# A state-space scan in pairs of chunks, with the matmuls of the scan in written order and its part-array products gathered

## The chip, the cores and the metric

The kernel runs on one core of a Trainium2 chip. The metric is device time in microseconds for one launch. The core's engines are TensorE (PE in the profile: matmuls, with PEld for the loading of weights), VectorE (DVE), ScalarE (ACT), GpSimd (POOL) and SyncE (SP, which issues most DMAs). Each engine works its own instructions off in the order in which they were issued, and waits on semaphores where it needs the result of another.

## The reference

One step of a small hybrid decoder: one Mamba-2 (SSD) layer, then one layer of causal pooling, then an RMSNorm. There are 1024 prompt tokens and 8 sampled sequences of 8 tokens, d_model is 1024, all in float32. The part that matters here is the SSD layer, cut:

```python
def ssd_scan(x, dt, A, B, C, h0):          # T = 128 tokens a chunk, 8 groups of 4 heads, D_STATE 128
    acum = jnp.cumsum(dt * A.reshape(G, R), axis=2)
    decay = jnp.where(mask, jnp.exp(acum[t] - acum[s]), 0.0)
    CB = einsum(C, B); xdt = x * dt
    y_intra = einsum(CB * decay, xdt)                       # inside a chunk
    chunk_states = einsum(B, exp(acum[-1] - acum), xdt)     # S: what a chunk adds to the state
    h = exp(acum[-1]) * h + chunk_states                    # from chunk to chunk
    y_inter = einsum(C, exp(acum), h_prev)                  # from the state before
    return y_intra + y_inter, h_final

def ssd_branch(h, ...):
    z, xbc, dt_raw = split(h @ w_in)
    xs, Bm, Cm = split(silu(conv_b + sum(xp[:, k:k + L] * conv_w[k] for k in range(4))))
    y, new_ssm = ssd_scan(xs, softplus(dt_raw + dt_bias), -exp(a_log), Bm, Cm, ssm_prev)
    gated = (y + d_skip * xs) * silu(z)
    gated = gated * rsqrt(mean(gated * gated over the 256 channels of a group) + EPS) * norm_g
    return gated @ w_out, ...
```

The pooling layer has another silu(z) gate. Both layers take their shift, scale and gate from `silu(c) @ ada_w` (adaLN).

## The kernel before

Activations lie transposed, 128 channels on the partitions and the 1088 tokens (1024 prompt, 64 sample) along the free axis. A float32 product is made as three products of the form float32r: weights and activations are split into a high part (a copy on ScalarE) and a low part (a subtraction on VectorE). Small products in the scan are plain float32, which the hardware does in two passes, so each stands twice in the profile.

**Stages.** `front` norms the input, makes some z, B, C and x projections, and the dt terms (`dt_phase`). `ssd_layer` then runs the scan of the 8 groups g, one after the other, and between their steps the projections of the next group: 4 tiles (B, C, and two of x) of 3 token ranges each, 12 units of 24 matmuls (`proj_group`, `mm1`, L174 to L176). After each tile follow the conv of 4 taps and the silu (`conv_tile`, L340 to L348), written as x/2 * (1 + tanh(x/2)). `ssd_out` and `pool_layer` follow; their large products are made in the seven products of Strassen's scheme.

**The scan of a group** (`scan_group`). For each of 8 chunks, `front(c)` transposes x and B (L534), makes C·B (L530), the decay matrix M (ScalarE Relu L541 and Exp L542, VectorE L545), xd (x times dt, and times the decay to the chunk's end, L547) and C times exp(acum) (ea, L560). `back(c)` makes y (L575 and, from the state before, L579), and the state: S (L582) goes to PSUM, GpSimd multiplies the state before by the decay (hd, L588), and VectorE adds S (L589; for the first chunk a copy, L585). The row of cumulated decays, spread over the partitions, comes by DMA (acb, two buffers). After the chunks come the sample tokens: Z (L603) with the cached states, y (L616, L619), and the new states (`state_sample`: L640, L641 into the PSUM tile S or y, L643 adds on VectorE). Then the gate: y * silu(z) (L671), squares on ScalarE (L672), their sum (L673), the norm's mean by products with ones (L681), Ln and Exp, a trip through DRAM to spread it over the partitions, and the scaling (L693).

**Part of the array.** y, Z, the mean, the sample's transposes (`dup`, L422) and the adaLN products (L245) use 64 or 32 columns of the array with a tile position; two or four of them run side by side. Transposes, C·B, S, the sample's new states and the projections use all of it.

**PSUM.** There are eight banks: mm three, tr two, y two, S one.

```python
S = pp.tile([P, 512], F32, tag="S", bufs=1, name=self.name("S"))                                   # back(c)
S = pp.tile([P, 512], F32, tag=("S", "y")[b2 % 2], bufs=1 + b2 % 2, name=self.name("S"))           # state_sample
```

**Order.** The code is traced once; a planner then orders each engine's instructions by when their inputs are ready in its own plan and, among ready ones, by the order of tracing. It may put a matmul that is traced later ahead of one that waits. In `ssd_layer` a loop gives the tracing order: one step of the scan, one unit of projection.

```python
for g in range(7):
    G = self.proj_open(g + 1)
    sc, pr = self.scan_group(g, T), self.late(self.proj_group(G), sc)
    T = G["out"]
    if g < 6:
        self.weave(itertools.islice(sc, 11), pr, (1, 1, 1, 1, 1, 1, 1, 1, 1, 1, 2))
```

With the last group the units are those of the output product (`out_units`, L1139 to L1141, 24 matmuls of 272 columns a unit).

ScalarE's functions need a table; Exp and Ln share one, tanh is loaded again in turn (L299, L345).

## Time and profile before

| | |
|---|---|
| median of 3 timed runs | 1656.93 us (1655.12 to 1659.39) |
| span of the profiled execution | 1652.6 us |
| TensorE busy | 1606.9 us, 97% |
| VectorE, ScalarE, GpSimd busy | 1348.5, 852.7, 482.3 us |
| DMA | 272.35 MB, mean 165 GB/s |
| mean granted TensorE clock | 0.993 |

The profile gives the profiled execution no time of its own beside its span; the timed runs lie 2.5 to 6.8 us above that span. Rows of a group read: line, engine, operation, output <- inputs, shapes, count | busy us, mean ns of one | idle of the engine before them, and what ended it. A row of the windows: window, its length, then for each engine busy us (and instructions), granted clock, DMA share, GB/s. A row in order of time: start, length, engine, line, operation; in brackets idle time before it and what ended it. A TensorE instruction's length includes its way through the array, so the cost of one in a stream is the distance of the starts. A line number is that of the kernel before.

### The profile page before, as it was taken

The numbers are of one execution on the slowest core, as the hardware profiler recorded it, in microseconds if no ns is written. First come the engines' busy times: TensorE is split into PE (matmuls) and PEld (weight loads), VectorE is DVE, ScalarE is ACT, GpSimd is POOL, SyncE is SP. The second block draws the span as 40 slices with busy tenths as digits, with TensorE's granted clock in tenths as the row PEclk, the third lists the DMA queues.
The fourth block names the chain that finished last, engine by engine and source line by source line (L and its number), as shares of the span: only waits on it lengthen the run. The fifth ranks groups of instructions, "written<-read, shape, count | busy, mean of one in ns | idle before, by whom it ended". The sixth has DMA issues, their size and how long they took to land. (4 is left out here: it accounts for less than half of the span.)

```text
span 1652.6 us, 31547 instructions
## 1 busy us (share of the span) xinstructions
PE 1606.9 (97%) x12255; PEld 1516.0 (92%) x12255; DVE 1348.5 (82%) x2303; ACT 852.7 (52%) x1651; POOL 482.3 (29%) x517
## 2 busy tenths in 40 slices
PE   8999999999999999999888999999999999999997
PEld 6899999888888989888777999999999999999997
DVE  5897587788888787878888988979999878577876
ACT  6544335767676666767665356633332334233364
POOL 0124441213121313223221122256667640000241
PEclk8999999999999999999999999999999999999999
DMA  8423226445555454538897983133323369556773
GB/s 341 161 75 114 85 76 218 135 145 173 161 168 175 148 162 133 173 119 243 260 284 233 240 201 124 56 111 113 112 93 103 126 203 379 168 152 181 163 166 121
DMA packets 120837, 272.35 MB, mean 165 GB/s; under 512 B 18256, under 2 KB 58608, under 8 KB 120688
## 3 DMA queue, kind: packets, MB, share of 16 engines
q1 hardware_dynamic: 112624, 244.91, 44.2%
q0 software_dynamic: 8064, 25.43, 8.5%
q8 instruction: 96, 1.57, 0.4%
q14 instruction: 53, 0.43, 0.1%
HBM read 208.99 MB, written 56.86 MB: 161 GB/s over the span
## 5 line engine op out<-in xcount | busy, mean ns | idle before, releaser
L1139 PE MATMUL op<-b,w 128*128 128x272 f32 x896 | 259.5, 291 | 6.6 <-ACT w L1099 4.3
L1141 PE MATMUL op<-b,w 128*128 128x272 f32 x896 | 259.5, 291 | 3.2 <-DVE w L1100 3.0
L1140 PE MATMUL op<-b,w 128*128 128x272 f32 x896 | 259.2, 290 | 3.4 <-DVE b L1040 3.4
L174 PE MATMUL mm<-hh,wh 128*128 128x364 f32 x720 | 248.8, 346 | 0.0
L175 PE MATMUL mm<-hl,wh 128*128 128x364 f32 x720 | 238.6, 331 | 0.0
L176 PE MATMUL mm<-hh,wl 128*128 128x364 f32 x720 | 237.5, 330 | 0.0
L888 PE MATMUL st<-hh,w 128*128 128x272 f32 x704 | 203.5, 289 | 0.5 <-DVE w L168 0.5
L887 PE MATMUL st<-hl,w 128*128 128x272 f32 x704 | 203.3, 289 | 0.0
L886 PE MATMUL st<-hh,w 128*128 128x272 f32 x704 | 203.1, 288 | 0.0
L1139 PEld LDWEIGHTS op<-b,w 128*128 128x128 f32 x896 | 169.4, 190 | 8.6 <-ACT w L1099 5.0
L1140 PEld LDWEIGHTS op<-b,w 128*128 128x128 f32 x896 | 169.4, 189 | 6.0 <-DVE b L1040 4.1
L1141 PEld LDWEIGHTS op<-b,w 128*128 128x128 f32 x896 | 169.3, 189 | 4.9 <-DVE w L1100 4.2
L888 PE MATMUL st<-t,w 128*128 128x272 f32 x528 | 152.3, 288 | 2.8 <-POOL w L168 2.0
L887 PE MATMUL st<-t,w 128*128 128x272 f32 x528 | 152.2, 288 | 0.7 <-DVE t L1331 0.7
L588 POOL TENSOR_TENSOR hd<-h,cd 128x256 f32<-128x256 f32 x56 | 76.5, 1367 | 261.2 <-DVE h L589 147.3
L886 PE MATMUL st<-t,w 128*128 128x272 f32 x528 | 151.9, 288 | 0.0
L174 PEld LDWEIGHTS mm<-hh,wh 128*128 128x128 f32 x720 | 135.4, 188 | 6.0 <-ACT raw L404 2.5
L175 PEld LDWEIGHTS mm<-hl,wh 128*128 128x128 f32 x720 | 135.5, 188 | 4.2 <-issue 2.7
L342 DVE SCALAR_TENSOR_TENSOR raw<-raw,cwh,raw 128x1112 f32<-128x1112 f32 x96 | 133.0, 1385 | 6.9 <-ACT raw L340 6.4
L176 PEld LDWEIGHTS mm<-hh,wl 128*128 128x128 f32 x720 | 135.3, 188 | 3.0 <-issue 2.9
L886 PEld LDWEIGHTS st<-hh,w 128*128 128x128 f32 x704 | 132.9, 189 | 0.3 <-issue 0.3
L888 PEld LDWEIGHTS st<-hh,w 128*128 128x128 f32 x704 | 132.5, 188 | 0.7 <-DVE w L168 0.7
(289 smaller groups left out, 4208.4 us busy)
## 6 DMA issues: line engine op xcount, KB each, us to landing
wr<-win SPq DMA_DIRECT2D x48, 512.0 KB, 3.7
acb<-acd SPq DMA_DIRECT2D x64, 256.0 KB, 4.3
wr<-pin SPq DMA_DIRECT2D x32, 512.0 KB, 3.9
wr<-wout SPq DMA_DIRECT2D x28, 512.0 KB, 7.8
wr<-pout SPq DMA_DIRECT2D x28, 512.0 KB, 4.2
row<-gyd SPq DMA_DIRECT2D x22, 544.0 KB, 7.9
wr<-wout POOLq DMA_DIRECT2D x20, 512.0 KB, 8.4
wr<-pout POOLq DMA_DIRECT2D x20, 512.0 KB, 5.5
```

The lines of the kernel that those rows point to most:

```text
L174: nc.tensor.matmul(ps[:, :n], hi[:, k, :], ah[:, a:a + n], start=first, stop=False)
L175: nc.tensor.matmul(ps[:, :n], hi[:, k, :], al[:, a:a + n], start=False, stop=False)
L176: nc.tensor.matmul(ps[:, :n], lo[:, k, :], ah[:, a:a + n], start=False, stop=last)
L342: nc.vector.scalar_tensor_tensor(out=acc[:, :n], in0=raw[:, k:k + n], scalar=w[k], in1=acc[:, :n], op0=ALU.mult, op1=ALU.add)
L588: nc.gpsimd.tensor_tensor(out=hd, in0=h, in1=cd.unsqueeze(2).to_broadcast([P, 4, 64]), op=ALU.mult)
L886: nc.tensor.matmul(ps[c][:, :QUART], hi[:, k], xh[:, t], start=(k == 0), stop=False)
L887: nc.tensor.matmul(ps[c][:, :QUART], hi[:, k], xl[:, t], start=False, stop=False)
L888: nc.tensor.matmul(ps[c][:, :QUART], lo[:, k], xh[:, t], start=False, stop=(k == 3))
L1139: nc.tensor.matmul(ps[:, :QUART], hi[:, k], xh, start=k == 0, stop=False)
L1140: nc.tensor.matmul(ps[:, :QUART], hi[:, k], xl, start=False, stop=False)
L1141: mm = nc.tensor.matmul(ps[:, :QUART], lo[:, k], xh, start=False, stop=k == 7)
```

## The change

The scan works on pairs of chunks: 4 steps p of 256 tokens instead of 8 of 128. Its transposes, M, ea, xd, S and y are made for both chunks at once (M and ea 128 x 1024, one tile px for x, one pb for B and C·B); acb is one buffer of twice the size. `scan_front(p + 1)` is issued before the step p.

Every matmul traced in `ssd_layer` is pinned behind the one traced before it on TensorE, so the planner can't reorder them. Each step issues whole-array products first and then all that use a part of the array: y, then the sample's products or the mean, then an adaLN block. The projections of the next group run 3 units ahead (`LEAD`), and `PACE` says how many units stand at three places of each step.

The conv's last tap writes the result directly, and a silu on ScalarE is applied in place, in a burst for all four tiles of a group at the end of a scan; the gates' tanh and multiplication become one silu. The sum of the squares is taken by the products with ones (two sets of them) instead of VectorE. The scale 0.5 and its helper tiles go. The x tiles of the first output product are loaded one by one.

```diff
+LEAD = 3
+PACE = (((1, 1, 1), (0, 1, 2), (0, 1, 2), (0, 1, 2)),) * 6 + (((1, 1, 1), (0, 1, 2), (0, 2, 2), (0, 2, 4)), ((1, 1, 1), (0, 1, 1), (0, 1, 1), (0, 1, 1)))
...
+    def pin(self, ins):
+        return self.build.tc.keep_in_program_order(ins) if self.build.pinned else ins
...
-        for k in range(1, 4):
+        for k in range(1, 3):
             nc.vector.scalar_tensor_tensor(out=acc[:, :n], in0=raw[:, k:k + n], scalar=w[k], in1=acc[:, :n], op0=ALU.mult, op1=ALU.add)
+        nc.vector.scalar_tensor_tensor(out=dst[:, :NP], in0=raw[:, 3:3 + NP], scalar=w[3], in1=acc[:, :NP], op0=ALU.mult, op1=ALU.add)
...
-        nc.scalar.activation(raw[:, :n], acc[:, :n], AF.Tanh)
-        nc.vector.scalar_tensor_tensor(out=dst[:, :NP], in0=raw[:, :NP], scalar=1.0, in1=acc[:, :NP], op0=ALU.add, op1=ALU.mult)
...
+    def silu_burst(self, ts):
+        for t in ts:
+            self.tab(self.nc.scalar.activation(t, t, AF.Silu))
+        self.tab(self.nc.scalar.preload_act_table_set("natural_log_exp_and_others"))
...
+    def scan_state(self, s, p):
+        S = self.pp.tile([P, 512], F32, tag="S", bufs=1, name=self.name("S"))
+        for cc in range(2):
+            self.te.matmul(S[:, 256 * cc:256 * cc + 256], Bt[:, cc], xd[:, cc, 1].rearrange("p r q -> p (r q)"), start=True, stop=True)
+        for cc in range(2):
+            h, Sv = s.h[-1], S[:, 256 * cc:256 * cc + 256].rearrange("p (r q) -> p r q", r=4)
+            if h is None:
+                nc.vector.tensor_copy(hn, Sv)
             else:
+                nc.gpsimd.tensor_tensor(out=hd, in0=h, in1=cd[:, :, cc].unsqueeze(2).to_broadcast([P, 4, 64]), op=ALU.mult)
+                nc.vector.tensor_tensor(out=hn, in0=hd, in1=Sv, op=ALU.add)
...
+    def sample_state(self, s, half):
+        for i in range(2):
+            S = self.pp.tile([P, 512], F32, tag=("S", "y")[i], bufs=1 + i, name=self.name("S"))
+            self.te.matmul(S, Bt[:, 0], xm, start=True, stop=False)
+            self.te.matmul(S, Bt[:, 1], xm, start=False, stop=True)
+            self.nc.vector.tensor_tensor(out=d, in0=d, in1=S, op=ALU.add)
...
+    def gate_norm(self, s):
+        for q in range(2):
+            for j in range(4):
+                self.te.matmul(ps[32 * j:32 * j + 32, :272], self.ones[:, :32], sq[q][:, 272 * j:272 * j + 272], start=(q == 0), stop=(q == 1), tile_position=(0, 32 * j))
...
-        t = self.mt.tile([P, 416], F32, tag="mt", bufs=2, name=self.name("zt"))
-        nc.scalar.activation(t[:, :n], src, AF.Tanh, scale=0.5)
-        return nc.vector.scalar_tensor_tensor(out=dst[:, a:a + n], in0=t[:, :n], scalar=1.0, in1=src, op0=ALU.add, op1=ALU.mult)
+        return self.nc.scalar.activation(dst[:, a:a + n], src, AF.Silu)
...
+    def scan(self, s, fill):
+        for p in range(4):
+            a, b, c = PACE[g][p]
+            if p == 0 and g == 7:
+                self.sample_state(last, 0)
+            self.units(fill, a)
+            if p < 3:
+                self.scan_front(s, p + 1)
...
+            self.scan_state(s, p)
+            if last and p == 0 and g < 7:
+                self.sample_state(last, 0)
+            self.units(fill, b)
+            self.scan_y(s, p)
+            if p == 3:
+                self.sample_y(s)
+            if p == 2:
+                self.sample_front(s)
+                self.sample_inter(s)
+            if last and p == 1:
+                self.gate_norm(last)
+            ada = self.ada(g, p)
+            next(ada, None)
+            if last and p == 0:
+                self.sample_state(last, 1)
...
+            elif p == 3:
+                if g < 6:
+                    self.silu_burst(after.T)
+                self.sample_prep(s)
...
+            self.units(fill, min(c, 1))
...
+            self.units(fill, c - min(c, 1))
+            if p == 3 and after:
...
+                self.scan_front(after, 0)
+                self.scan_ac(after, 1)
+                self.gate_rows(s)
```

## The prediction

> **What bounds the kernel now.** I read the page first, then the sums by window, then the order of TensorE's instructions in the scan, and last the rows of the operations that the change moves.

> ```profile
> span 1652.6 us, 31547 instructions
> PE 1606.9 (97%) x12255; PEld 1516.0 (92%) x12255; DVE 1348.5 (82%) x2303; ACT 852.7 (52%) x1651; POOL 482.3 (29%) x517
> 300.00:750.00 450.00, 450.00 (x3413) 397.77 (x3412) 359.46 (x599) 304.14 (x680) 108.94 (x161) 1.00 0.50 156
> 750.00:900.00 150.00, 133.71 (x1049) 118.68 (x1047) 130.62 (x227) 94.61 (x196) 38.03 (x38) 0.98 0.83 255
> ```

> TensorE (PE) is the bound. In the stage that the change rewrites, 300 to 750 us, it is busy for 450.00 of 450 us; VectorE (359.46) and ScalarE (304.14) have room. So two things can move the time: how long TensorE's own stream takes, and new waits inside it. Only the tail of the scan, 750 to 900 us, has idle time now, 16.3 us. The sum below is made against this execution, span 1652.6 us; the three timed runs have a median of 1656.93, 4.3 us more, which I add at the end.

> A busy PE hides what its instructions cost, so I look at their starts.

> ```profile
> 281.17 0.66 PE L575 MATMUL y<-M,xd 128*64 128x128 f32 x8
> 281.76 0.43 PE L175 MATMUL mm<-hl,wh 128*128 128x360 f32 x1
> ...
> 539.38 0.44 PE L575 MATMUL y<-M,xd 128*64 128x128 f32 x4
> ...
> 540.09 0.39 PE L579 MATMUL y<-ea,h 128*64 128x128 f32 x4
> 540.40 0.70 PE L582 MATMUL S<-xd,Bt 128*128 128x256 f32 x2
> ...
> 546.60 0.70 PE L582 MATMUL S<-xd,Bt 128*128 128x256 f32 x2
> 546.94 0.52 PE L174 MATMUL mm<-hh,wh 128*128 128x364 f32 x1
> 547.30 0.33 PE L175 MATMUL mm<-hl,wh 128*128 128x364 f32 x1
> ...
> 550.94 0.33 PE L176 MATMUL mm<-hh,wl 128*128 128x364 f32 x1
> 551.20 0.27 PE L530 MATMUL tr<-xbc,xbc 128*64 128x64 f32 x1
> ...
> 884.52 0.67 PE L681 MATMUL ms<-z,ones 128*32 128x272 f32 x8
> 885.12 0.39 PE L1140 MATMUL op<-b,w 128*128 128x272 f32 x1
> ```

> The form 128*64 or 128*32 marks a product on part of the array, 128*128 one on all of it. A part stretch of 8 products lasts from 281.17 to 281.76, 0.59 us; one of 16 (four groups of 4, the first and the last shown) from 539.38 to 540.40, 1.02 us. So a product costs 0.054 us, and each stretch 0.16 us that does not depend on its length. The whole-array stretch from 546.60 to 551.20 lasts 4.60 us. It holds 24 projection products at 0.165 us ((550.94 - 547.30) / 22), 3.97 us, and two 256-column passes at 0.215 us (four times 0.054), 0.43 us: 0.20 us are left over. A change of array form and back thus costs about **0.35 us** of TensorE in which nothing is computed, though the engine counts as busy. Between 281.17 and the last such stretch at 884.52 I count 117 part stretches, 14 to 16 for each of the 8 scans.

> **The change part by part.**

> *Four stretches a scan.* In each step of two chunks the change puts y, and whatever of the sample's products, the norm and the adaLN block is due, behind one another. That makes 32 stretches and one for the last norm, 33: 84 fewer, times 0.35 = **-29.4 us**. A quarter of a scan more or less is 2 stretches; bounds -26 and -33. Changes between 64 and 32 columns inside a stretch stay about as many as now (some 3 a scan); I take 0, bounds -2 and +3.

> *Norm.* The squares' sum moves from VectorE to TensorE: 8 more L681 products a scan. The stretch at 884.52 has 8 in 0.60 us, 0.45 without its change of form; 8 x 0.45 = **+3.6 us**, bounds 3 and 5.

> *Other products* (transposes, C·B, S, the sample's, the 84 projection units) stay in number and size: 0.

> *VectorE and ScalarE.*

> ```profile
> L342 DVE SCALAR_TENSOR_TENSOR raw<-raw,cwh,raw 128x1112 f32<-128x1112 f32 x96 | 133.0, 1385 | 6.9 <-ACT raw L340 6.4
> L346 DVE SCALAR_TENSOR_TENSOR xbc<-raw,raw 128x1024 f32<-128x1024 f32 x32 | 40.8, 1274 | 10.2 <-ACT raw L345 10.0
> L348 DVE SCALAR_TENSOR_TENSOR xbc<-raw,raw 128x64 f32<-128x64 f32 x32 | 6.9, 217 | 0.0
> L340 ACT ACTIVATE raw<-raw,cwh 128x1112 f32<-128x1112 f32 x32 | 42.1, 1315 | 1.8 <-DVE xbc L348 1.3
> L404 ACT ACTIVATE raw<-mm 128x364 f32<-128x364 f32 (+1 forms) x84 | 37.6, 449 | 53.7 <-PE mm L176 52.9
> L345 ACT ACTIVATE raw<-raw 128x1112 f32<-128x1112 f32 x32 | 36.2, 1131 | 23.4 <-DVE raw L342 23.3
> L299 ACT ACT_TABLE_LOAD x12 | 15.4, 1283 | 11.5 <-PE ms L681 11.4
> L673 DVE TENSOR_TENSOR z<-z,z 128x1088 f32<-128x1088 f32 x8 | 10.2, 1279 | 0.0
> L754 DVE SCALAR_TENSOR_TENSOR z<-zt,z 128x272 f32<-128x272 f32 x48 | 27.2, 572 | 9.6 <-ACT zt L753 9.5
> L754 DVE SCALAR_TENSOR_TENSOR pz<-zt,pz 128x272 f32<-128x272 f32 x56 | 24.5, 439 | 13.7 <-ACT zt L753 13.7
> ```

> The third full tap goes (32 x 1.385), L673 goes (10.2) and most of L754 goes (51.7 in these two groups): VectorE loses about 106 us. It hides behind TensorE, so the gain is 0, bounds -4 (short waits in the front and pool stages) and 0. ScalarE swaps a tanh for a silu at the same length and keeps about two table loads a scan: 0.

> *Burst against the next scan.* Scan g+1's first transposes need all four silus. From the end of a group's last projection unit to these transposes stand, by the prices above, S (1.1), a unit (4.0), y (1.9), the sample's y (0.9) and two units (8.0), 16 us. The chain is two evictions L404 0.9, L340 1.3, taps 2 x 1.385 + 1.274 + 0.217 = 4.3, table load 1.3, silu 1.1 = 8.9 us: hidden by 7 us; if VectorE is late it comes out into the open. Bounds 0 and +3 at each of 7 borders. The last border has two output units (6 us) instead: about 3 to 6 us, in place of waits that stand there now.

> *One buffer for S, and a fixed order.* Here I expect the loss. In the first step of scans 1 to 6 the code issues `scan_state(s, 0)` and right behind it `sample_state(last, 0)`. Both write the PSUM tile S, which has one buffer, and the matmuls can no longer pass each other. The second must wait until VectorE has copied the first state, GpSimd has decayed it, and VectorE has added the second one. Everything on TensorE is queued behind it. Now only the copy has to be awaited, and the order fills the time:

> ```profile
> 510.40 0.68 PE L582 MATMUL S<-xd,Bt 128*128 128x256 f32 x2
> 512.57 0.41 DVE L585 COPY h<-S 128x256 f32<-128x256 f32 x1
> 512.91 0.40 PE L640 MATMUL S<-xs,Bt 128*128 128x512 f32 x1
> 513.16 0.61 POOL L588 TENSOR_TENSOR hd<-h,cd 128x256 f32<-128x256 f32 x1 [11.56 <-DVE h L585]
> ...
> 587.75 0.42 DVE L585 COPY h<-S 128x256 f32<-128x256 f32 x1
> L585 DVE COPY h<-S x8: 410/417/425, 275.0 to 824.9; 128x256 f32<-128x256 f32 x8
> L588 POOL TENSOR_TENSOR hd<-h,cd x56: 612/932/2817, 281.7 to 865.7; 128x256 f32<-128x256 f32 x56
> L588 POOL TENSOR_TENSOR hd<-h,cd 128x256 f32<-128x256 f32 x56 | 76.5, 1367 | 261.2 <-DVE h L589 147.3 <-DVE h L585 76.8 <-ACT cd L559 23.6
> L589 DVE TENSOR_TENSOR h<-hd,S x56: 404/411/422, 287.8 to 870.1; 128x256 f32<-128x256 f32 x56
> ```

> S ends at 511.08 and the copy starts at 512.57, 1.5 us behind other VectorE work. Then 0.4 (copy), 0.2, 1.4 (mean of L588), 0.3 (half a mean VectorE operation, 1348.5 us / 2303), 0.4 (add), 0.1: 4.3 us, six times that is **+26 us**. Lower bound, with no queue and L588 at its shortest: 0.1 + 0.4 + 0.1 + 0.6 + 0.1 + 0.4 + 0.1 = 1.8, +11 us. Upper bound: L588 at 2.8 and the queue of 1.5 before both VectorE steps, 6.9, +41. I take the middle since at that moment VectorE holds a conv tile (4.3 us), M, ea, and the xd of two steps. `sample_state(last, 1)` then waits in the same step for the two y evictions (its other buffer holds the adaLN block): about 0.7 us, **+4**, bounds 0 and +16 (2.7 each).

> *The clock.* An idle of that length can cost more than itself:

> ```profile
> 824.19 0.58 PE L530 MATMUL tr<-xbc,xbc 128*128 128x128 f32 x1 [3.60 <-ACT Bt L551]
> 826.00:828.00 2.00, 2.00 (x17) 1.64 (x14) 2.00 (x5) 1.27 (x4) 0.88 (x1) 0.50 0.27 62
> 900.03 0.39 PE L1140 MATMUL op<-b,w 128*128 128x272 f32 x1 [3.07 <-DVE b L1040]
> 900.00:904.00 4.00, 3.97 (x30) 3.84 (x31) 4.00 (x7) 1.96 (x3) 1.66 (x2) 1.00 0.93 284
> ```

> After a wait of 3.60 us the granted clock is 0.50 in 826 to 828; after one of 3.07 us it stays 1.00. At half clock for some 4 us or more, 2 us or more are lost. My 4.3 us is a mean; I let half of the six stalls pay 2 us: **+6**, bounds 0 and +20. [...]

> *Tail.* Scan 7 now overlaps its step's front with the step before, so the waits of L530 on Bt (3.60 above) should go; but its acb is one buffer of 512 KB for two of 256 KB, reloaded only after ScalarE has read it:

> ```profile
> acb<-acd SPq DMA_DIRECT2D x64, 256.0 KB, 4.3
> ```

> If a load of twice the size lands in twice the time, 8.6 us, and that only after the reading, it fills the 10 us or so of a step with two output units, and the DMA share there is 0.83 already. I take 0, bounds -10 and +10.

> **Sum.** 1652.6 - 29.4 + 3.6 + 26 + 4 + 6 = 1662.8 of span; with 4.3, **1667 us**, 0.6% slower. Own range 1660 to 1676.

> **The rivals.**

> *Faster: the S chain is short.* VectorE is 106 us lighter and TensorE's halt lets it drain. At the lower bound, without y waits and clock: 1652.6 - 29.4 + 3.6 + 11 = 1637.8, **1642 us**. It decides from the point where a first step loses less than 25.8 / 6 = 4.3 us in all. For it: L588's shortest 0.61 us, and it was 0.61 in the row above. Against it: the copy's 1.5 us of queue.

> *No change.* First steps lose about 4.3 us, all in: **1657 us**, within 5 us of the time before. 0.3% is about what a measurement of this kernel tells from no change.

> *Much slower: every stall halves the clock.* Six times 3.4 us instead of +6, so +20: 1652.6 - 29.4 + 3.6 + 26 + 4 + 20 = 1677, **1681 us**; a burst that is late at the scan borders would give a like time. For it: 4.3 is above the 3.60 that fell. Against: 3.07 did not fall.

> *The change doesn't do what it says*: if a change of form cost nothing, the 25.8 us would be missing and the time be 1693. The rows of 8 and 16 products speak against it; I give it a part of the third rival.

> **How the numbers follow.** Forecast 0.37, faster 0.36, no change 0.12, much slower 0.15. The forecast is ahead by a hair, because the order is written down and the chain has three steps, while its length is an estimate. So faster by over 0.3% is 0.36, within 0.3% 0.13 (a little of the forecast's lower end), slower 0.51. The range runs from 1638 to 1687: below it lies about a third of the faster case, above it half of the much slower one.

> **What will show it.** Right: PE waits on "h" before the sample's S product in scans 1 to 6, 4 to 5 us each, some with a PEclk of 0.5 behind them; about 33 part stretches; VectorE near 1240 us busy. Wrong: no such wait, or below 3 us, and scans that follow each other faster than the 75.2 us of now (587.75 - 512.57) by nearly 4 us; or waits of transposes on silu, which would move the loss to the scan borders. If the tail from 750 us on loses much less than 16 us, my 0 for it was the error.

## The result, and the profile after

The changed kernel takes **1724.49 us** in the median of four runs (1723.92 to 1729.07), beside 1657.7 us for the kernel before: 1.0409 times as long, interval 1.0393 to 1.0425. The forecast was 1667 us with a range up to 1687, so the direction was right and the size far off. The profiled execution has a span of 1722.3 us, 69.7 more than before.

The page of the changed kernel:

```profile
span 1722.3 us, 30963 instructions
PE 1602.7 (93%) x12335; PEld 1536.5 (89%) x12335; DVE 1240.8 (72%) x1984; ACT 831.5 (48%) x1485; POOL 450.5 (26%) x516
```

Its waits of TensorE (what waited, its releaser, microseconds in all, how often, the longest):

```profile
PE S L98 <- DVE h L576: 45.4, 6, 7.9
PE y L98 <- DVE h L576: 29.3, 16, 3.9
PE tr L101 <- ACT xbc L394: 5.9, 1, 5.9
PE S L98 <- DVE h L699: 4.8, 1, 4.8
```

VectorE is 107.7 us lighter (106 were worked out), and TensorE busy 93% instead of 97%. (All of TensorE's products now stand in one line, L98; the sample's S product is "S<-xm", scan_state's "S<-xd".) The first two waits, which are new, make 74.7 us.

I sum TensorE's time over the whole execution from the trace and its clock records: idle time; time lost at half clock, an estimate: half of the time for which TensorE was busy at 0.50 (in the trace after, projection products start 0.305 us apart there and 0.166 us at full clock, output products 0.227 and 0.125, in the median, so the true loss is somewhat below half); and the rest, taken as what its instruction stream needs at full clock. The 4 us of the prediction for y's evictions stand under "all else", since they are another wait than y's on h.

| | before | after | difference | predicted |
|---|---|---|---|---|
| stream | 1597.5 | 1569.5 | -28.0 | -25.8 |
| idle: S on h | 0 | 45.4 | +45.4 | +26 |
| idle: y on h L576 | 0 | 29.3 | +29.3 | 0 |
| idle: all else | 45.7 | 44.9 | -0.8 | +4 |
| half clock | 9.4 | 33.2 | +23.8 | +6 |
| span | 1652.6 | 1722.3 | +69.7 | +10.2 |

One scan shows it in one row each. The windows run from a halt of S to the next in the kernel after, and from a copy to the next in the kernel before; the columns are start and end, length, busy time of PE, PEld, DVE, ACT and POOL with their instructions, granted clock, DMA share, GB/s. After:

```profile
456.92:542.57 85.65, 74.31 (x577) 69.05 (x577) 54.54 (x76) 48.89 (x100) 12.57 (x28) 0.96 0.42 136
```

Before:

```profile
512.57:587.75 75.18, 75.18 (x568) 66.72 (x567) 61.13 (x101) 51.42 (x116) 20.26 (x27) 1.00 0.49 155
```

A scan was 75.18 us, all of it busy at full clock. It is now 85.65, of which 11.3 us are idle and 2.3 are lost to the clock (74.31 busy; the sum of lost time gives a stream of 72.0).

**Where the halt comes from.** The timeline of the changed kernel around the first halt, first TensorE (start, length, engine, line, operation; in brackets the idle time before and its releaser):

```profile
361.27 1.03 PE L98 MATMUL S<-xd,Bt 128*128 128x256 f32 x4
369.95 2.04 PE L98 MATMUL S<-xm,Bs 128*128 128x512 f32 x4 [7.65 <-DVE h L576]
```

GpSimd:

```profile
368.73 0.61 POOL L575 TENSOR_TENSOR hd<-h,cd 128x256 f32<-128x256 f32 x1 [10.77 <-DVE h L572]
```

VectorE:

```profile
361.69 1.37 DVE L358 SCALAR_TENSOR_TENSOR raw<-raw,vec,raw 128x1112 f32<-128x1112 f32 x1
362.98 0.68 DVE L541 TENSOR_TENSOR xd<-tr,tkx 128x512 f32<-128x512 f32 x1
363.58 1.27 DVE L359 SCALAR_TENSOR_TENSOR xbc<-raw,vec,raw 128x1024 f32<-128x1024 f32 x1
364.77 0.28 DVE L361 SCALAR_TENSOR_TENSOR xbc<-raw,vec,raw 128x64 f32<-128x64 f32 x1
364.97 0.68 DVE L541 TENSOR_TENSOR xd<-tr,tkx 128x512 f32<-128x512 f32 x1
365.57 0.41 DVE L544 TENSOR_TENSOR cb<-tr,kc 128x256 f32<-128x256 f32 x1
365.90 1.22 DVE L558 TENSOR_TENSOR ea<-xbc,ea 128x1024 f32<-128x1024 f32 x1
367.03 1.22 DVE L557 TENSOR_TENSOR M<-M,cb 128x1024 f32<-128x1024 f32 x1
368.17 0.42 DVE L572 COPY h<-S 128x256 f32<-128x256 f32 x1
369.38 0.42 DVE L576 TENSOR_TENSOR h<-hd,S 128x256 f32<-128x256 f32 x1 [0.79 <-POOL hd L575]
```

S is done at 362.3. The copy that frees the bank starts at 368.17, **5.9 us** later, behind a convolution tile's taps, two xd, cb, ea and M. After that the chain is short: copy, 0.61 us of decay, add, 1.8 us in all until the next S product at 369.95. TensorE has nothing else to do in this time, because everything is queued behind S<-xm.

The wait of y has the same cause, one step on. TensorE:

```profile
393.07 0.44 PE L98 MATMUL y<-ea,h 128*64 128x128 f32 x4 [1.51 <-DVE h L576]
```

VectorE:

```profile
390.07 1.22 DVE L557 TENSOR_TENSOR M<-M,cb 128x1024 f32<-128x1024 f32 x1
391.21 1.28 DVE L359 SCALAR_TENSOR_TENSOR xbc<-raw,vec,raw 128x1024 f32<-128x1024 f32 x1
392.40 0.28 DVE L361 SCALAR_TENSOR_TENSOR xbc<-raw,vec,raw 128x64 f32<-128x64 f32 x1
392.60 0.41 DVE L576 TENSOR_TENSOR h<-hd,S 128x256 f32<-128x256 f32 x1
```

y needs the state that the step's first chunk adds, one projection unit (4.0 us) stands between S and y, and the add is queued behind M and the taps. Steps 1 and 2 of each scan lose some 1.5 us so, and the last steps up to 3.9.

### The profile page after: what moved, and what is told of

Read it like the earlier page. It is cut to its first block, busy times and chain, and to the rows that moved or that the text cites. A ratio compares the mean times of both kernels' runs of the same rounds, so it can differ in the third digit from the quotient of the medians.

```text
span 1722.3 us, 30963 instructions
## 1 busy us (share of the span) xinstructions
PE 1602.7 (93%) x12335; PEld 1536.5 (89%) x12335; DVE 1240.8 (72%) x1984; ACT 831.5 (48%) x1485; POOL 450.5 (26%) x516
## 4 chain that ended last, share of the span: by engine, by line
PE 68%; DVE 13%; ACT 7%; issue 6%; DMA 5%; POOL 2%; SPq 0%; DVEq 0%; POOLq 0%; ACTq 0%
PE st L98 27%; PE mm L98 18%; PE op L98 13%; DVE raw L358 3%; PE pl L98 3%; DVE xbc L359 2%; PE y L98 2%; PE am L98 2%; PE S L98 1%; ACT M L553 1%; DVE M L557 1%; DVE xd L541 1%; PE ms L98 1%; DMA row<-gyd 1%; DVE wl L153 1%
## 5 line engine op out<-in xcount | busy, mean ns | idle before, releaser
L98 PE MATMUL op<-b,w 128*128 128x272 f32 x2688 | 353.8, 293 | 11.9 <-ACT w L1136 5.9
L98 PEld LDWEIGHTS op<-b,w 128*128 128x128 f32 x2688 | 347.1, 192 | 18.7 <-ACT w L1136 6.6
L98 PE MATMUL st<-hh,w 128*128 128x272 f32 x1408 | 273.8, 289 | 0.0
L98 PE MATMUL mm<-hh,wh 128*128 128x364 f32 x720 | 247.1, 343 | 0.1
L98 PE MATMUL mm<-hl,wh 128*128 128x364 f32 x720 | 239.2, 332 | 0.0
L98 PE MATMUL mm<-hh,wl 128*128 128x364 f32 x720 | 238.6, 331 | 0.0
L98 PEld LDWEIGHTS st<-hh,w 128*128 128x128 f32 x1408 | 224.6, 188 | 0.3 <-issue 0.3
L98 PE MATMUL st<-t,w 128*128 128x272 f32 x1584 | 205.3, 287 | 0.0
L98 PE MATMUL st<-hl,w 128*128 128x272 f32 x704 | 203.4, 289 | 0.0
L98 PEld LDWEIGHTS st<-t,w 128*128 128x128 f32 x1584 | 201.0, 188 | 0.0
L98 PEld LDWEIGHTS mm<-hh,wh 128*128 128x128 f32 x720 | 138.1, 192 | 9.2 <-issue 6.7
L98 PEld LDWEIGHTS mm<-hl,wh 128*128 128x128 f32 x720 | 137.8, 191 | 1.4
L98 PEld LDWEIGHTS mm<-hh,wl 128*128 128x128 f32 x720 | 137.6, 191 | 0.0
L98 PEld LDWEIGHTS st<-hl,w 128*128 128x128 f32 x704 | 132.6, 188 | 0.0
L553 ACT ACTIVATE M<-acb,tka 128x128 f32<-128x128 f32 x256 | 83.0, 390 | 37.6 <-PE y L98 34.8
L1156 DVE SCALAR_TENSOR_TENSOR x<-op,gat,x 128x272 f32<-128x272 f32 (+1 forms) x160 | 72.7, 477 | 37.7 <-PE op L98 31.6
L1136 ACT ACTIVATE w<-wr 128x1024 fp32r<-128x1024 f32 x56 | 59.1, 1055 | 80.7 <-PE op L98 57.6
L358 DVE SCALAR_TENSOR_TENSOR raw<-raw,vec,raw 128x1112 f32<-128x1112 f32 x64 | 87.7, 1371 | 7.7 <-ACT raw L356 7.2
L575 POOL TENSOR_TENSOR hd<-h,cd 128x256 f32<-128x256 f32 x56 | 41.1, 734 | 197.9 <-DVE h L576 111.5
```

What stands on the lines that cost most here:

```text
L98: return self.pin(self.build.nc.tensor.matmul(*a, **k))
L358: nc.vector.scalar_tensor_tensor(out=acc[:, :n], in0=raw[:, k:k + n], scalar=w[k], in1=acc[:, :n], op0=ALU.mult, op1=ALU.add)
L553: nc.scalar.activation(M[:, r, t], acb[:, r, t], AF.Relu, bias=self.tka[cc][:, col + r:col + r + 1], scale=-1.0)
L575: nc.gpsimd.tensor_tensor(out=hd, in0=h, in1=cd[:, :, cc].unsqueeze(2).to_broadcast([P, 4, 64]), op=ALU.mult)
L1136: self.nc.scalar.activation(hi, r, AF.Copy)
L1156: ins = nc.vector.scalar_tensor_tensor(out=x[e][:, a:a + pn], in0=ps[:, :pn], scalar=g, in1=x[e][:, a:a + pn], op0=ALU.mult, op1=ALU.add)
```

## The experiments

The theory after the traces: TensorE's products can no longer pass each other, so each step of VectorE on which a product depends must be on time; the two places where it is not are the shared bank S and the single unit ahead of y. The rivals: VectorE's backlog itself is the loss, wherever the waits stand; or gathering the part-array products brought nothing, and the stream changed for another reason. The kernel before took 1657.45 us beside the first four kernels, 1658.1 beside the others.

### 1. The sample's product first

```diff
-            if p == 0 and g == 7:
+            if last and p == 0:
                 self.sample_state(last, 0)
...
-            if last and p == 0 and g < 7:
-                self.sample_state(last, 0)
```

> The changed kernel, with one line moved: in step 0 of scans 1 to 6 the sample's first new state is issued before the projection unit and scan_state, as it is in scan 7. Nothing is left out. Theory A (one S buffer in a fixed order): the six waits of 7.6 us on VectorE's second state go, 45 us, and the half clock behind them, about 1.8 us each, 11 us. But the chain copy, decay, add starts 5 us late behind VectorE's other work, so y of step 0, one unit (4 us) behind, should now wait 2 to 4 us: 6 x 3 = 18 us come back. 1724 - 45 - 11 + 18 = 1686 us. Theory B (the state chain itself is too late, whoever reads it): the wait moves to y whole, but for the unit between, so 7.6 - 4 = 3.6 us each: 1724 - 45 + 22 = 1701 or, with the clock kept up, 1690. The trace tells them apart: under A the wait is on the copy (the first state) alone, under B on the added state too.

Measured: 1684.12 us, 1.0152 of before (1.0123 to 1.0182), 40 us less than the change. The waits of TensorE:

```profile
PE y L98 <- DVE h L576: 30.7, 17, 4.4
PE y L98 <- DVE h L572: 11.0, 7, 1.9
```

The halts of S are gone. Some of the same lateness comes back where step 0's y waits for the copy (L572) alone, 11.0 us, as theory A said; its time was 1686.

### 2. Another bank, the same order

```diff
-            S = self.pp.tile([P, 512], F32, tag=("S", "y")[i], bufs=1 + i, name=self.name("S"))
+            S = self.pp.tile([P, 512], F32, tag=("mm", "y")[i], bufs=3 - i, name=self.name("S"))
```

> The changed kernel with its order kept: only the sample's first new state goes to a buffer of the tag mm (three of them) instead of S (one). Nothing is left out. Theory A (the shared buffer makes the wait): the six waits of 7.6 us go without any move, time about as in the run before, 1680 to 1695 us. Rival (the order, or the sample's operands xm and Bs, are late): the wait stays at 5 us or more, time 1715 to 1725.

Measured: 1683.11 us, 1.0149 (1.0108 to 1.0191).

```profile
PE y L98 <- DVE h L576: 34.0, 16, 5.1
```

With the order as it was and only the bank changed the halts of S are gone too. So the one buffer, in the written order, is what made them.

### 3. Two units between the state and y

```diff
-PACE = (((1, 1, 1), (0, 1, 2), (0, 1, 2), (0, 1, 2)),) * 6 + (((1, 1, 1), (0, 1, 2), (0, 2, 2), (0, 2, 4)), ...)
+PACE = (((1, 2, 1), (0, 2, 1), (0, 2, 1), (0, 2, 0)),) * 6 + (((1, 2, 1), (0, 2, 1), (0, 2, 2), (0, 2, 3)), ...)
```

The second number of a step is the units between its state and its y. The order of the adaLN weights' loads was shifted to fit.

> The changed kernel with two projection units instead of one between scan_state and y of a step, and one fewer after y (12 a scan as before; the adaLN blocks' weights are queued to match). The S order is kept. Nothing is left out. Theory: the waits of y on the added state (1.5 us twice a scan and 3.9 us once, 29 us in all) go, the 45 us of S stay: 1724 - 25 = 1699 us. Rival: VectorE is simply behind by more than a unit, and waits of 1 us or more stay in y: 1710 to 1720.

Measured: 1699.67 us, 1.0249 (1.0207 to 1.0292).

```profile
PE S L98 <- DVE h L576: 36.6, 7, 6.0
PE y L98 <- DVE h L576: 9.2, 3, 6.1
```

The waits of y in the steady scans are gone; what is left of them lies in the tail. The unit that was missing is worth 25 us of time. Of y's waits 20.1 us go, not 25, and the halts of S shrink too (5.95 us for 7.65 at the first); a new wait of tr on xd (5.3 us in all) takes some of it back.

### 4. The first and the third together

> Both edits: the sample's first new state ahead of scan_state, and two units between scan_state and y. Nothing is left out. If the two waits are all that went wrong in scans 1 to 6: 1724 - 45 - 25 - 11 (clock) = 1643 us, faster than the kernel before by about 0.9%, since the gathered part-array products then show their 28 us. If the gathering brings nothing and only the waits count, it ends at 1657 us or above.

Measured: 1670.4 us, 1.0069 (1.0048 to 1.009): 27 us too slow for what I expected. A wait has come in that the changed kernel had once, in its tail, and now five of the scans have:

```profile
PE S L98 <- DVE h L699: 15.4, 5, 3.1
```

Now scan_state's S finds its bank taken by the sample's product of step 0, whose add is late by the same queue. These two cures do not add up, and both products still share the bank.

### 5. The second and the third together

> Both cures at once, the order left as the change has it: sample_state(last, 0) stays behind scan_state in the first step of scans 1 to 6 but takes its first tile from another bank, and two projection units stand between each state and its y. Theory A (the shared buffer and the unit that is missing ahead of y are the loss, VectorE's backlog harms only through them): against the run with two units alone (1699.7 us) its 36.6 us of S waits go, and about 10 us of lost clock, 1653 us, and the waits of S on the sample's add that kept the run with both cures at 1670 (15.4 us) do not appear. Theory B (VectorE is late by the same amount wherever the product is put, a wait of about 3 us a scan comes back at another place): 1665 to 1672 us with a new wait on VectorE of 3 us in each of scans 1 to 6.

Measured: 1650.46 us, **0.9939** (0.992 to 0.9958). This version, with every product still in the written order, is 0.6% faster than the kernel before. Its page (span 1645.8 us):

```profile
PE 1588.5 (97%) x12335; PEld 1525.9 (93%) x12335; DVE 1242.8 (76%) x1984; ACT 832.4 (51%) x1485; POOL 487.0 (30%) x516
```

Its largest wait in scans 1 to 6, in total:

```profile
PE tr L101 <- DVE xd L541: 5.3, 5, 1.1
```

One scan, in a window:

```profile
584.05:656.90 72.85, 71.79 (x576) 66.87 (x577) 55.31 (x77) 48.92 (x100) 18.78 (x27) 1.00 0.47 160
```

A scan takes 72.85 us for 75.18 before, 71.79 of them busy, at full clock. Theory A's number (1653) holds, B's (1665 to 1672) does not; of B's returning wait 1.1 us a scan is there.

### 6. The same pace in scan 7

```diff
-                  ... ((1, 1, 1), (0, 1, 1), (0, 1, 1), (0, 1, 1)))
+                  ... ((1, 2, 0), (0, 2, 0), (0, 2, 0), (0, 2, 0)))
```

> As the run before, and in scan 7 two output units between each state and its y too (the same nine units, none behind y). Theory A: the waits of y on h in scan 7 (2.9 + 6.2 us with both earlier cures) go and 8 us are gained, 1645 us. Theory B: the output units come when their rows are not yet there, TensorE waits for b instead, and nothing is gained, within 3 us of the run before.

Measured: 1652.99 us, 0.9962 (0.9941 to 0.9983), no better than the run before: theory B. The y wait of 6.8 us goes, and longer waits of output units on b (up to 3.7 us) and one of S on x (3.0) come instead.

### 7. Each y in two halves

```diff
-            self.units(fill, b)
-            self.scan_y(s, p)
+            self.units(fill, b - 1)
+            self.scan_y(s, p, fill)
...
         for cc in range(2):
+            self.units(fill, cc)
             h, t = s.h[2 * p + cc], slice(128 * cc, 128 * cc + 128)
```

> As the first run of this set, but each step's y in two halves with the second projection unit (or scan 7's output unit) between them: 32 part-array stretches more, not one instruction more. Theory A (a change between part and whole array costs 0.35 us in the instruction stream): +11 us against the first run of this set, all of it in the stream and none of it idle. Theory B (gathering brought nothing, the 28 us that the stream lost came from elsewhere): 0 to 2 us.

Measured: 1671.83 us, 1.0068 (1.0051 to 1.0085), 21 us more than run 5. TensorE has 12335 instructions as in run 5. A scan at full clock:

```profile
512.37:589.47 77.10, 73.55 (x577) 66.86 (x577) 55.40 (x77) 48.56 (x100) 18.16 (x27) 1.00 0.44 151
```

The part stretches rise from 33 to 65 with no instruction added. A scan's busy time at full clock rises from 71.79 to 73.55, 0.44 us for each of its four new stretches; over the whole kernel the stream rises from 1569.4 to 1580.8, 11.4 us, **0.36 us** a stretch. That is the price predicted, and theory B is out. What the spans differ by beside that (24.7 in all) was not expected: 7.4 us of idle time and 5.9 of clock. The wait of tr on xd grows to 1.9 us a scan and one of S on zsc comes in.

### 8. The changed kernel in free order

```diff
-        return self.build.tc.keep_in_program_order(ins) if self.build.pinned else ins
+        return self.build.tc.keep_in_program_order(ins) if False else ins
```

> The changed kernel with TensorE's products not held in the order written, nothing else. Theory A (the fixed order makes the late buffer a halt): the scheduler moves other products ahead of the sample's S and of the y that waits, so S waits fall below 15 us in all and y waits below 15; the part stretches become more, some 50 to 70 for 33 (0.35 us each, 6 to 13 us back), 1665 to 1690 us. Theory B (VectorE's backlog binds whatever the order): S waits as before, 1715 to 1725 us.

Measured: 1640.78 us, **0.9879** (0.986 to 0.9898): 84 us less than the change, and 1.2% less than before. Theory A's mechanism holds, with 58 part stretches and 1.1 us of waits of S and none of y on h left; its time, 1665 to 1690, was too long. The same place in the scan, TensorE:

```profile
357.76 1.03 PE L98 MATMUL S<-xd,Bt 128*128 128x256 f32 x4
358.43 0.82 PE L98 MATMUL S<-xm,Bs 128*128 128x512 f32 x2
359.09 0.33 PE L98 MATMUL mm<-hh,wh 128*128 128x364 f32 x1
...
363.16 0.88 PE L98 MATMUL y<-M,xd 128*64 128x128 f32 x12
363.96 0.43 PE L98 MATMUL mm<-hh,wh 128*128 128x360 f32 x1
```

VectorE:

```profile
364.03 0.42 DVE L572 COPY h<-S 128x256 f32<-128x256 f32 x1
```

The copy is as late as in the changed kernel: S is done at 358.8, it starts at 364.03, 5.2 us later. But TensorE makes, of the sample's tiles, the one in the other bank, then a projection unit, the y products that need no new state, and the next unit. **Nearly the same delay of VectorE, 5.9 us in the written order and 5.2 in the free one, costs TensorE 7.65 us in the first and nothing in the second.** The price is 58 part stretches for 33: the stream is 10.0 us longer than after the change, 0.40 us for each of the 25, and idle time falls from 119.6 to 42.6 us, lost clock from 33.2 to 18.7.

### 9. Free order and both cures

> Free order and both cures (other bank for the sample's first S tile, two units between state and y). Theory A (with the cures the scheduler has less reason to break stretches up): part stretches fall from 58 to some 35 to 45, 5 to 8 us of stream less than with the free order alone (1640.8 us): 1634 us. Theory B (the free order already hides all that the cures hide, and its breaks come from elsewhere): 1638 to 1644 us.

Measured: **1634.31 us**, 0.9857 (0.9833 to 0.9881), the fastest of all. Part stretches fall to 39 and the stream to 1570.9 us, theory A.

```profile
300.00:740.00 440.00, 437.69 (x3526) 410.24 (x3525) 336.73 (x470) 296.86 (x608) 109.41 (x162) 1.00 0.49 158
```

In 440 us of scans TensorE is idle for 2.3.

### 10. Free order in scan 7 alone

```diff
         for s in self.scans:
+            self.pinned = s.g < 7
             self.scan(s, fill)
```

with both cures and the written order in scans 0 to 6. What follows scan 7 in `ssd_layer` is free too.

> Written order in scans 0 to 6, free order in scan 7 alone, both cures. Theory A (order is what makes the tail's waits too): between scan 7's start and the last norm the idle time of 20 us falls to the 14 us of the free order, and 1 to 2 us of clock with it, 1643 us for 1650.5. Theory B (the tail waits for data that no order brings earlier): 1648 to 1652 us.

Measured: 1648.52 us (1641.11 to 1651.79), 0.9936 (0.991 to 0.9961), the same as run 5 and theory B's time. Its reason is not shown: y's waits on h fall from 8.3 to 2.6 us, as theory A has it, and idle time in all from 57.3 to 54.2. But the stream grows by 2.9 us, with 37 part stretches for 33. So the free order has in part exchanged waits for stretches here.

### 11. Fewer taps on VectorE

```diff
-        for k in range(1, 3):
-            nc.vector.scalar_tensor_tensor(out=acc[:, :n], in0=raw[:, k:k + n], scalar=w[k], in1=acc[:, :n], ...)
```

> The changed kernel without the two full taps of each convolution on VectorE (L358, 64 x 1.37 us; they are left out, so the convolution is not the reference's). Theory A (the halt is VectorE's queue ahead of the copy: one or two taps of 1.37 us stand in it): S waits fall from 7.6 to 5 to 6 us each (45 to some 32 us), y's waits of 1.5 us mostly go, 1690 to 1700 us. Theory B (the halt is the chain copy, decay, add itself): S and y waits stay within 5 us of 75 us, 1717 to 1725 us.

Measured: 1671.81 us, 1.0078 (1.0051 to 1.0104), 53 us less than the change, more than either theory gave. The waits:

```profile
PE S L98 <- DVE h L574: 24.4, 7, 4.2
```

VectorE and GpSimd at the place of the first halt:

```profile
358.14 0.41 DVE L570 COPY h<-S 128x256 f32<-128x256 f32 x1
358.47 1.21 DVE L555 TENSOR_TENSOR M<-M,cb 128x1024 f32<-128x1024 f32 x1
358.70 1.46 POOL L573 TENSOR_TENSOR hd<-h,cd 128x256 f32<-128x256 f32 x1 [6.84 <-DVE h L570]
360.19 0.42 DVE L574 TENSOR_TENSOR h<-hd,S 128x256 f32<-128x256 f32 x1 [0.51 <-POOL hd L573]
```

The copy now comes 0.8 us after S, and the halt is 3.4 us for 7.65. The queue ahead of the copy has lost 5.1 us, while the chain from the copy to the next S has grown from 1.8 to 2.6: the decay, now beside M, takes 1.46 us for 0.61, and the add waits for it. So most of the halt was what VectorE had to do ahead of the copy, and 3.4 us of copy, decay and add stay.

### 12. A third tap back, in free order

```diff
-        for k in range(1, 3):
+        for k in (1, 2, 2):
```

> The changed kernel in free order with a third full tap on VectorE in each convolution, as much work as the kernel before had there (32 x 1.37 = 44 us; the tap is added a second time, so the convolution is not the reference's). Theory A (VectorE's relief lies beside TensorE, the prediction's 0): within 4 us of the free order's 1640.8. Theory B (the relief is what lets the free order run without waits): 1648 to 1670 us.

Measured: 1655.64 us, 0.9986 (0.9968 to 1.0004), 15 us more than the free order with the lighter VectorE. VectorE is busy for 1289.2 us, 78% of the span. The largest wait in the scans, in total:

```profile
PE y L98 <- DVE h L576: 7.6, 5, 2.1
```

44 us of VectorE work, on an engine idle for 22% of the span, cost 15 us of time: theory B. The profiled executions differ by 17.7 us: 7.0 of idle time, 9.3 of stream and 1.4 of clock. There are 69 part stretches for 58. 11 stretches at 0.36 make 4 us of the 9.3; where the other 5 come from stays open.

## Why the prediction was wrong

**The stream** was right. 33 part stretches were predicted and are there, and with the norm's added products the stream lost 28.0 us for 25.8. The price of 0.35 us a stretch, taken from two rows of the kernel before, came out at 0.36 when 32 stretches were put back (run 7). The rival in which a change of form costs nothing falls with it.

**Three steps failed.** The span grew by 59.5 us more than the sum says. A term put at nothing is 29.3 of them, the halt at the bank S 19.4, the clock 17.8; the stream and the waits that were summed and did not come give 7.0 back.

**The halt at S: the right mechanism, mis-sized.** The place, the six scans and the chain were as predicted, but each halt took 7.6 us (45.4 / 6), not 4.3, and more than the upper bound of 6.9. Two entries were wrong in opposite directions. The copy's queue was 5.0 to 6.0 us in the six scans, not 1.5. The 1.5 is the kernel before's, in six of its scans; the changed kernel's copy is 5.0 to 6.0 us late in free order too (run 8), so it is not the written order that makes it late; the order only makes TensorE pay. Run 11 ties the lateness to the work ahead of the copy, the taps above all. Decay and add were shorter, 1.8 us from the copy's start for some 2.8. The prediction had named what VectorE holds at that moment ("a conv tile (4.3 us), M, ea, and the xd of two steps") and still not summed it: the conv tile alone is more than twice the 1.5. Without two taps of each convolution the halt is 3.4 us.

**A term was missing**: y's wait for the state that the step's own first chunk adds, 29.3 us. The sum has nothing for it. Its 4 us for y are another wait, for an eviction, which the trace does not show. One more unit ahead of y takes away 20.1 of the 29.3 (run 3).

**The clock**: I let half of the six stalls pay 2 us; all six did, and the whole is +23.8 us for +6. The trace's clock records have 6.83 us at 0.50 at each of the six. The window over the first of them, and the sum of the windows over all six:

```profile
365.91:372.74 6.83, 2.79 (x8) 2.44 (x9) 4.47 (x7) 0.00 (x0) 1.23 (x2) 0.50 0.17 59
sum 40.98, PE 24.62 PEld 22.50 DVE 18.67 ACT 0.00 POOL 7.38; mean PE 4.10 PEld 3.75 DVE 3.11 ACT 0.00 POOL 1.23
```

The clock falls while TensorE still waits (365.91, the halt ends at 369.95), and there it costs nothing. TensorE was busy for 24.62 of these 41 us, so 12.3 us are lost by the estimate of the table, 2.1 at a stall: the 2 us were right, the half was wrong. The third rival's condition held, that every stall halves the clock; its price of 3.4 us each did not, and its time, 1681, fell short by the missing terms. 3.4 us is half of the 6.83 us for which the clock was at 0.50 behind the wait of 3.60 us in the kernel before (823.42 to 830.25), and neither the trace before nor the one after shows it lost at one stall: TensorE was busy for 6.06 of those 6.83 us, 3.0 lost, and at the six stalls for 2.79 to 4.56, 1.4 to 2.3 lost. Another 7.0 us more than before were lost in the tail, and the rest nearly all behind the scans.

**VectorE's relief at 0** was wrong. Work that lies beside a busy TensorE still sets when a state is ready; 44 of the 106 us are worth 15 us in the free order (run 12); no run puts the tap back in the written order. The reason "it hides behind TensorE" looked at shares of busy time, not at the chain of h from step to step.

**The faster rival** (the chain is short, VectorE drains) named 1642 us. The changed kernel in free order takes 1640.8, but that is luck: the rival has the written order and a short chain, and run 8 has neither. What the change holds beside the written order is worth 17 us; the written order took 84. With the bank and the pace mended, the written order costs some 14 to 16 us against the free one (runs 5 and 9).

**Scan borders and tail.** The silus were hidden at six borders, as worked out. At the last one they came out into the open for 5.9 us (I had 3 to 6), in place of waits that were there before:

```profile
PE tr L530 <- ACT Bt L551: 7.0, 4, 3.6
```

These went, as predicted. But the tail got the y waits of up to 3.9 us and the wait of S on the sample's add (4.8) besides. From the first copy of scan 6 to the last norm the kernel before is idle for 13.2 us and loses 3.0 to the clock; the changed kernel, from its last halt to the last norm, 23.0 and, beside that halt's own, 10.0. My 0 was too low. The load of acb did not show among the waits: its 512 KB land in 4.5 us on the page after, not in the 8.6 that I feared. Runs 6 and 10 did not mend the tail, and what sets it was not settled.

## What to carry to other kernels

Writing an in-order engine's order down can turn a lateness of the other engines into a halt. Before it is done, list for each product what it reads and whose bank it takes, and sum what the engine that must deliver will have queued in front of that in the new kernel; do not take the wait seen in the old one. What a delay costs under a free order is no measure of its cost under a fixed one: here 5.2 us of lateness cost nothing, and 5.9 us cost 7.65 and 1.4 of clock. Give two products that meet in a fixed order two banks, and put more work between a state and its reader than the slowest queue holds.

## What the runs showed of the hardware

A change from whole to part array and back cost TensorE 0.36 us in the stream of the whole kernel and 0.44 us in a scan at full clock, in which it counts as busy (run 7; 0.40 in run 8).

```profile
354.25:357.66 3.41, 1.85 (x14) 1.39 (x12) 3.41 (x5) 1.50 (x3) 0.00 (x0) 1.00 0.44 134
357.66:361.07 3.41, 1.76 (x9) 1.66 (x10) 3.39 (x5) 3.41 (x9) 0.00 (x0) 1.00 0.10 40
361.07:364.48 3.41, 3.41 (x23) 3.41 (x22) 2.60 (x3) 2.43 (x8) 0.00 (x0) 1.00 0.28 114
...
593.18:596.59 3.41, 0.66 (x6) 0.47 (x4) 3.41 (x4) 2.21 (x3) 0.00 (x0) 1.00 0.07 25
596.59:600.00 3.41, 3.08 (x8) 2.72 (x9) 2.59 (x6) 3.41 (x10) 0.00 (x0) 0.50 0.37 154
```

A border of the grid divides the first wait, and each of its two steps is busy for more than half; the third lies nearly whole in one step, busy for 0.66 us, and the next step has half clock. Run 7 has five waits of 1.93 us: three lie in one step and are followed by half clock, two are divided and are not. Over the fourteen traces, each from its first half-clock stretch on, of the steps at full clock none of 6241 with less than 1.16 us idle was followed by half clock, all 90 with more than 1.96 us were, and 32 of the 160 between.

The waits of 3.60 and 3.07 us in the kernel before, of which the first was followed by half clock and the second was not, fit this too: 2.8 us of the first lie in one step, and the second is divided into halves of 1.5. So in these runs waits below 3.6 us halved the clock too, down to 1.93 us, and whether one of 1.93 or of 3.08 us did went with where it fell on the grid.
